# A two-layer decoder trunk: half of the low parts of the FFN output weights are subtracted on GpSimd instead of VectorE

## The chip, the cores and the metric

The kernel runs on one core of a Trainium2 chip. The metric is the device time of one execution in microseconds, as the median of several runs. One execution was also taken by the hardware profiler, and all rows below come from it. The engines are called as in the profile: PE is TensorE (PEld its weight loads), DVE is VectorE, ACT is ScalarE, POOL is GpSimd, SP is SyncE, whose queue (SPq) issues the loads of weights.

## The reference

256 tokens of 1024 fp32 values pass through two layers. Each layer is half an FFN, a token mixer, and half an FFN again, each with a norm before and a norm after it and added to the residual. The mixer of the first layer is stick-breaking attention, that of the second latent attention. The FFN is the part that the change touches:

```python
def swiglu(x, w_in, w_out):
    gate, up = jnp.split(x @ w_in, 2, axis=-1)
    return (jax.nn.silu(gate) * up) @ w_out
...
    for i in range(DEPTH):
        g = norm_g[i]
        f = swiglu(rms_norm(x, g[0]), ffn_w_in[i, 0], ffn_w_out[i, 0])
        x = x + FFN_RESIDUAL_WEIGHT * rms_norm(f, g[1])
        ...
        f = swiglu(rms_norm(x, g[4]), ffn_w_in[i, 1], ffn_w_out[i, 1])
        x = x + FFN_RESIDUAL_WEIGHT * rms_norm(f, g[5])
```

`w_in` is 1024 by 5632, `w_out` 2816 by 1024, all in fp32. There are four FFNs.

## The kernel before

**Pieces.** Every weight is read once from HBM, in the order in which it is used, into one of four raw tiles of 128 by 1024 fp32 (`RAWS`; `load`, line 329; the queue is SyncE's, its loads are line 334). A raw tile holds two pieces, 128 rows of a weight by 512 columns. ACT rounds a piece to fp32r, its high part (`nc.scalar.copy`, line 345); DVE subtracts that from the raw values, which gives the low part (`low`, line 351). A raw tile is free for the next load when both subtractions are done. High and low parts lie in `r` tiles, of which there are 76.

**Products.** For each piece PE does three products of 512 columns: high by high, high by low and low by high (`mm3`, line 476; the product itself is line 474). The tokens are two blocks of 128, and each uses every piece, so a piece is used by two times three products. Block 0 goes ahead of block 1 by at most `LEADS` pieces (14 in the first FFN), and at most `CAPS` pieces are held split (28 there).

**The FFN** (`ffn`, line 617). The inner dimension goes in 11 steps j of 256. For a step PE sums 8 pieces of gate and up columns into one bank. ACT does the silu (line 634), DVE multiplies it by the up half (line 636, the tile is `w`, called `hid` in the source), PE transposes that (line 482), ACT and DVE split it (lines 492 and 512), and the output rows of step j - 1 are added to two accumulator banks. The output rows of a step are 256 rows of `w_out`: two raw tiles of 128 rows by 1024 columns, and so four pieces, with key `("out", l, f, j, k, n)`, where k is the half of the rows and n the half of the columns. `add_rows` makes them in the order (k, n) = (0, 0), (0, 1), (1, 0), (1, 1); only the last group of all goes by n first.

**Norms.** POOL does little: constants at the start, four memsets, some copies in the latent attention, and the power -1/2 of each norm on one column (line 544; `rpre` for the norm ahead of a sub-layer, `rpost` for that behind it). Behind `rpost` DVE adds to the residual (line 581) and PE transposes the result for the next sub-layer (line 482).

**The order.** Nothing is ordered at run time. `Plan` records operations with their engine, a duration that the author gave, a class, and what they read and write. `run` then does a list schedule: an engine takes the operation that can start first, class 0 ahead of class 1 (the splits and the piece products are of class 1). The order that comes out is the program; each engine works through its own queue in that order, and waits at an instruction until what it reads is there and what it writes is free. A changed duration or engine can thus move instructions anywhere behind it.

Of the kernel before, what the change touches and what calls it, by code (L numbers as in the profile page):

```python
# [41 lines left out]
# For each sub-layer: how many pieces the first block of tokens may lead by, how many may be held.  # L42
# [14 lines left out]
# Durations, in microseconds, by which the order of the instructions is chosen.  # L57
# [23 lines left out]
class Buf:  # L81
    """A tile of a pool; it takes a slot with its first operation and gives it back after its last."""
# [17 lines left out]
class Plan:  # L100
    """Operations with what they read and write; run() emits them in the order of a list schedule."""
# [39 lines left out]
    def alt(self, o, eng, us, fn):  # L141
        """Another engine that may take the operation."""
        o.alt[eng] = (us, fn)
# [13 lines left out]
    def bank_ready(self, o, eng):  # L157
        """Two engines never access one bank at the same time."""
        w = 0.0
        for b in o.bufs:  # L160
            if b.tag == "bank":
                for e, end in b.touch.items():
                    if e != eng:
                        w = max(w, end + CROSS)
        return w
# [90 lines left out]
class Piece:  # L256
    """128 rows of a weight by up to 512 of its columns: the moving operand of three matrix products."""
# [7 lines left out]
def trunk(ctx: ExitStack, tc: tile.TileContext, x, positions, norm_g, ffn_w_in, ffn_w_out,  # L265
# [19 lines left out]
    # ---------------------------------------------------------------- constants  # L285
# [23 lines left out]
    # The tensor engine's clock rises with use: it is kept busy until the first operands are there.  # L309
# [14 lines left out]
    # ---------------------------------------------------------------- stream of weights  # L324
# [4 lines left out]
    def load(loads):  # L329
        """loads: (view of the raw tile, source, bytes)."""  # L330
# [8 lines left out]
    def split(raw, key, off, n, ks):  # L339
# [13 lines left out]
        op("dve", dve_us(n), low, r=rr + [(pc.hi, 0)], w=[(pc.lo, 0)], cls=1)  # L353

    def add(loads, parts):
        """parts: (key, offset, columns, loads it reads)."""
# [15 lines left out]
    def add_in2(kind, w, c0, c1, n):  # L372
        """[1024, n] at c0 beside [1024, n] at c1."""
# [50 lines left out]
    # ---------------------------------------------------------------- the tokens, and the gains of the norms  # L424
# [47 lines left out]
    # ---------------------------------------------------------------- helpers  # L472
# [11 lines left out]
    def act_hi(dst, src, n, r, w, scale=None, fast=False):  # L484
        """A copy, rounded, by ACT, or from SBUF (fast) by whichever engine is free first; dst, src: functions
        that give the access patterns once the buffers are placed."""
# [31 lines left out]
    def split_halves(dst, n, src, r):  # L518
        """src to both halves of a 512-column buffer: high part, low part."""
# [17 lines left out]
    def rstd(srcs, ss, ms, r, scale, eps, cls=0):  # L537
        """srcs: two functions giving halves of 512 columns, with what they read."""
# [8 lines left out]
    def pre_norm(b, l, i):  # L547
        """Gives x * gain, transposed, in two parts; the norm's factor, one per token, goes to rpre."""
# [36 lines left out]
    def use(b, key, fn, o, r, n):  # L585
        """The products of one piece of a weight."""
# [8 lines left out]
    def project(b, key, width):  # L595
        """[tokens, width] of x @ w, without the norm's factor."""
# [10 lines left out]
    def out_rows(b, key, t, acc, first, last, by_half=False):  # L607
        """acc += t^T @ w for 256 rows of w; t: a buffer of high and low parts."""
# [7 lines left out]
    # ---------------------------------------------------------------- FFN  # L616
# [35 lines left out]
    # ---------------------------------------------------------------- stick-breaking attention  # L652
# [3 lines left out]
    def tiles(b):  # L656
        """A bank of scores for four heads, or for two: (pair of heads, block of keys)."""
# [140 lines left out]
    # ---------------------------------------------------------------- rotary tables  # L798
# [8 lines left out]
    def rope_tables():  # L807
        """cos and sin of position * frequency: the angle in turns, taken apart so that every product
        whose whole turns are dropped is exact."""
# [327 lines left out]
```

## Time and profile before

| | |
|---|---|
| median of 2 runs | 970.34 us (970.26 to 970.42) |
| span of the profiled execution | 968.2 us; what lies around the span is not in the profile (the runs are 2.1 us longer) |
| granted TensorE clock, mean | 0.999 of full speed |
| HBM read | 168.15 MB, 175 GB/s over the span |

The span goes from the first to the last instruction. An idle time is put down to the engine that ended it, by the semaphores. Starts of instructions are good to the hundredth of a microsecond or so; the ends of products are modelled, since PE works on several at a time, so a product seems longer (some 390 ns) than the distance to the next one.

### The profile page before, as it was taken

How to read it: one execution, taken by the hardware profiler on the slowest of the kernel's cores; microseconds unless marked ns; L12 is line 12 of the kernel's file. 1: busy time of each engine (PE TensorE's matmuls, PEld its weight loads, DVE VectorE, ACT ScalarE, POOL GpSimd, SP SyncE). 2: the span in 40 equal slices, each digit the busy share in tenths (PEclk: the TensorE clock that was granted, in tenths of full speed). 3: DMA queues.
4: the chain of work that ended last, by engine and by line, in shares of the span. 5: the costliest groups of instructions: out<-in, count | busy, mean ns of one | idle time of the engine just before them, and what ended most of it. 6: DMA issues, size and time to landing. Idle time of an engine off the chain costs nothing.

```text
span 968.2 us, 13457 instructions
## 1 busy us (share of the span) xinstructions
PE 956.9 (99%) x4575; PEld 797.1 (82%) x4575; DVE 643.3 (66%) x1214; ACT 562.7 (58%) x1202; POOL 26.2 (3%) x75
## 2 busy tenths in 40 slices
PE   8999999999999999999999999999999999999997
PEld 6778888888888888888888888888899988888885
DVE  7884646678777875645477564556899997555533
ACT  7754535568878764545364453545798776444421
POOL 2000000000000000000000000000200000000000
PEclk9999999999999999999999999999999999999999
DMA  8885665634434385656745656575614178666511
GB/s 276 280 249 184 193 199 184 207 131 153 131 109 153 112 276 176 193 180 188 225 131 174 190 184 192 179 232 168 192 41 131 32 236 278 196 194 188 186 62 44
DMA packets 127974, 170.10 MB, mean 176 GB/s; under 512 B 8768, under 2 KB 109472, under 8 KB 127904
## 3 DMA queue, kind: packets, MB, share of 16 engines
q1 hardware_dynamic: 127792, 169.18, 55.2%
q8 instruction: 36, 0.59, 0.3%
q14 instruction: 34, 0.28, 0.1%
q10 hardware_dynamic: 112, 0.05, 0.0%
HBM read 168.15 MB, written 1.05 MB: 175 GB/s over the span
## 4 chain that ended last, share of the span: by engine, by line
PE 92%; DMA 3%; DVE 2%; ACT 1%; issue 1%; POOL 0%; SPq 0%; DVEq 0%; POOLq 0%; ACTq 0%
PE bank L474 88%; PE bank L482 5%; DMA raw<-in_ffn_w_in_dram 3%; DVE r L351 2%; ACT r L345 1%; SPq L334 0%; DVE w L636 0%; DVE w L559 0%; ACT r L492 0%; DVE x L581 0%; DVEq L1133 0%; ACT junk L540 0%; POOLq L1133 0%; POOL cbuild L299 0%; POOL invf L818 0%
## 5 line engine op out<-in xcount | busy, mean ns | idle before, releaser
L474 PE MATMUL bank<-r,r 128*128 128x512 f32 (+3 forms) x4080 | 926.2, 384 | 0.3 <-ACT r L345 0.2
L474 PEld LDWEIGHTS bank<-r,r 128*128 128x128 f32 (+1 forms) x4080 | 736.7, 188 | 139.5 <-ACT r L345 1.2
L351 DVE TENSOR_TENSOR r<-raw,r 128x512 fp32r<-128x512 f32 (+1 forms) x628 | 400.1, 683 | 42.4 <-ACT r L345 33.1
L345 ACT CAST r<-raw 128x512 fp32r<-128x512 f32 (+1 forms) x628 | 353.9, 616 | 56.8 <-DMA raw<-in_ffn_w_in_dram 26.7
L634 ACT ACTIVATE w<-bank,rpre 128x256 f32<-128x256 f32 x88 | 41.7, 474 | 215.5 <-PE bank L474 215.4
L636 DVE SCALAR_TENSOR_TENSOR w<-bank,rpre,w 128x256 f32<-128x256 f32 x88 | 42.5, 483 | 185.9 <-ACT w L634 185.9
L492 ACT CAST r<-bank 128x256 fp32r<-128x256 f32 (+5 forms) x166 | 64.2, 399 | 75.6 <-PE bank L482 65.7
L512 DVE TENSOR_TENSOR r<-bank,r 128x256 fp32r<-128x256 f32 (+5 forms) x166 | 74.3, 454 | 45.8 <-ACT r L492 44.7
L482 PE MATMUL bank<-ident,w 128*128 128x128 f32 (+1 forms) x326 | 55.0, 272 | 2.1 <-DVE w L636 2.0
L482 PEld LDWEIGHTS bank<-ident,w 128*128 128x128 f32 (+1 forms) x326 | 41.3, 137 | 16.6 <-DVE w L636 4.0
L512 DVE TENSOR_TENSOR r<-w,r 128x512 fp32r<-128x512 f32 x48 | 32.5, 687 | 4.9 <-ACT r L507 2.0
L540 ACT ACTIVATE junk<-bank 128x512 bf16<-128x512 f32 x24 | 14.3, 597 | 22.6 <-PE bank L474 22.5
L578 DVE TENSOR_TENSOR w<-bank,w 128x512 f32<-128x512 f32 x24 | 16.4, 684 | 15.9 <-ACT junk L540 15.7
L544 POOL TENSOR_TENSOR rpost<-ms,half_neg 128x1 f32<-128x1 f32 x12 | 6.6, 548 | 700.0 <-DVE ms L542 700.0
L559 DVE TENSOR_TENSOR w<-bank,gT 128x512 f32<-128x512 f32 x24 | 16.3, 686 | 2.2 <-PE bank L482 2.0
L540 ACT ACTIVATE junk<-x 128x512 bf16<-128x512 f32 x24 | 15.1, 631 | 4.3 <-DVE x L581 2.3
L581 DVE SCALAR_TENSOR_TENSOR x<-w,rpost,x 128x512 f32<-128x512 f32 x24 | 17.1, 745 | 0.4
L482 PE MATMUL bank<-ident,x 128*128 128x128 f32 x96 | 15.0, 297 | 0.0
L482 PEld LDWEIGHTS bank<-ident,x 128*128 128x128 f32 x96 | 12.9, 155 | 1.9 <-issue 0.2
L492 ACT CAST r<-w 128x512 fp32r<-128x512 f32 x20 | 12.2, 619 | 3.6 <-DVE w L559 3.5
L1035 ACT ACTIVATE w<-bank,mx 128x128 f32<-128x128 f32 (+1 forms) x32 | 13.1, 425 | 0.4 <-DVE mx L1031 0.3
L736 DVE SCALAR_TENSOR_TENSOR w<-bank,w 128x512 f32<-128x512 f32 x12 | 8.2, 689 | 4.3 <-ACT w L734 4.1
(85 smaller groups left out, 211.5 us busy)
## 6 DMA issues: line engine op xcount, KB each, us to landing
raw<-in_ffn_w_in_dram SPq DMA_DIRECT2D x352, 256.0 KB, 3.9
raw<-in_ffn_w_out_dram SPq DMA_DIRECT2D x88, 512.0 KB, 4.3
raw<-in_sb_w_in_dram SPq DMA_DIRECT2D x32, 256.0 KB, 3.6
raw<-in_sb_w_in_dram SPq DMA_DIRECT2D x8, 512.0 KB, 4.7
raw<-in_sb_w_out_dram SPq DMA_DIRECT2D x8, 512.0 KB, 3.3
raw<-in_mla_w_out_dram SPq DMA_DIRECT2D x8, 512.0 KB, 3.9
w<-in_norm_g_dram SPq DMA_DIRECT2D x12, 256.0 KB, 4.8
raw<-in_mla_w_in_dram SPq DMA_DIRECT2D x4, 416.0 KB, 3.6
```

Of the source, the lines that this page charges most:

```text
L345: h = op("act", act_us(n), lambda: nc.scalar.copy(pc.hi[:, :n], raw[:, off:off + n]), r=rr, w=[(pc.hi, 0)], cls=1, after=splits[-1:], piece=i)
L351: nc.vector.tensor_tensor(out=pc.lo[:, :n], in0=raw[:, off:off + n], in1=pc.hi[:, :n].bitcast(F32), op=ALU.subtract)
L474: nc.tensor.matmul(o, a, b, start=start, stop=stop, skip_group_check=True)
L482: nc.tensor.transpose(o, i, ident[:])
L492: nc.scalar.copy(dst(), src())
L512: nc.vector.tensor_tensor(out=dst(), in0=src(), in1=hi().bitcast(F32), op=ALU.subtract)
L540: op("act", act_us(512, 1), lambda src=src, h=h: nc.scalar.activation(junk[:], src(), AF.Square, scale=scale, accum_out=ss[:, h:h + 1]), r ...
L559: op("dve", dve_us(512), lambda h=h, y=y, tr=tr: nc.vector.tensor_tensor(out=y[:].rearrange("p (k t) -> p k t", t=P), in0=tr[:].rearrange( ...
L578: op("dve", dve_us(512), lambda h=h, t=t: nc.vector.tensor_mul(out=t[:], in0=acc[h][:], in1=g[h][:]), r=[(acc[h], 0), (g[h], 0)], w=[(t, 0 ...
L581: op("dve", dve_us(512) + 0.06, lambda h=h, t=t: nc.vector.scalar_tensor_tensor(xt[b][h][:], t[:], k.rpost[:], xt[b][h][:], op0=ALU.mult, ...
L634: op("act", act_us(FT, 1), lambda o=o, hid=hid: nc.scalar.activation(hid[:, 0:FT], o[:, 0:FT], AF.Silu, scale=k.rpre[:]), r=[(o, 0), (k.rp ...
L636: op("dve", dve_us(FT) + 0.06, lambda o=o, hid=hid: nc.vector.scalar_tensor_tensor(hid[:, FT:], o[:, FT:], k.rpre[:], hid[:, 0:FT], op0=AL ...
```

## The change

In `split`, a piece whose key begins with `out` and ends with 1, that is the second half of the columns of the FFN output rows, gets its low part from POOL: the same subtraction on the same tiles, given to the planner with 1.4 us instead of `dve_us(512)`, which is 0.60 us, in the same class. Output rows of the two attentions have other keys and stay as they were. Comments and docstrings go too, so lines behind line 351 move by six; nothing else changes.

```diff
         def low():
             nc.vector.tensor_tensor(out=pc.lo[:, :n], in0=raw[:, off:off + n], in1=pc.hi[:, :n].bitcast(F32),
                                     op=ALU.subtract)
-        op("dve", dve_us(n), low, r=rr + [(pc.hi, 0)], w=[(pc.lo, 0)], cls=1)
+        def low_pool():
+            nc.gpsimd.tensor_tensor(out=pc.lo[:, :n], in0=raw[:, off:off + n], in1=pc.hi[:, :n].bitcast(F32),
+                                    op=ALU.subtract)
+        if key[0] == "out" and key[-1] == 1:
+            op("pool", 1.4, low_pool, r=rr + [(pc.hi, 0)], w=[(pc.lo, 0)], cls=1)
+        else:
+            op("dve", dve_us(n), low, r=rr + [(pc.hi, 0)], w=[(pc.lo, 0)], cls=1)
```

On DVE, the first group of output rows stood like this before (lines 351 are the subtractions, `r43` to `r48` the low parts of the group from `raw0` and `raw1`, line 512 the split of `hid`, line 636 the next `hid`):

```order
L512 TENSOR_TENSOR r37_98<-bank2_152,r37_98 128x256
L351 TENSOR_TENSOR r39_100<-raw3_149,r36_97 128x512
L351 TENSOR_TENSOR r41_102<-raw3_149,r38_99 128x512
L351 TENSOR_TENSOR r43_104<-raw0_146,r40_101 128x512
L351 TENSOR_TENSOR r45_106<-raw0_146,r42_103 128x512
L351 TENSOR_TENSOR r47_108<-raw1_147,r44_105 128x512
L351 TENSOR_TENSOR r48_109<-raw1_147,r46_107 128x512
L636 SCALAR_TENSOR_TENSOR w7_144<-bank1_151,rpre0_198,w7_144 128x256
```

Now DVE has this there (`rt` are small steps of the rotary tables; lines are six higher behind line 351):

```order
L518 TENSOR_TENSOR r37_98<-bank2_152,r37_98 128x256
L351 TENSOR_TENSOR r39_100<-raw3_149,r36_97 128x512
L351 TENSOR_TENSOR r41_102<-raw3_149,r38_99 128x512
L351 TENSOR_TENSOR r43_104<-raw0_146,r40_101 128x512
L836 TENSOR_SCALAR rt9_232<-rt8_231 128x32
L837 TENSOR_SCALAR rt4_227<-rt4_227 128x32
L837 TENSOR_SCALAR rt9_232<-rt9_232 128x32
L847 SCALAR_TENSOR_TENSOR rt5_228<-rt4_227,rt3_226 128x32
L351 TENSOR_TENSOR r47_108<-raw1_147,r45_106 128x512
L842 TENSOR_SCALAR rt11_234<-rt4_227 128x32
L847 SCALAR_TENSOR_TENSOR rt22_245<-rt4_227,rt21_244 128x32
L642 SCALAR_TENSOR_TENSOR w7_144<-bank1_151,rpre0_198,w7_144 128x256
```

The second subtraction of each of the two raw tiles is gone from DVE, and steps of the rotary tables that stood further back have taken their room.

On POOL, at the change from the second FFN to the third (501 to 513 us in the trace of before), the powers of the two norms of both blocks stood one behind the other before. Now subtractions stand between them (lines 550 are the powers, line 354 the subtractions):

```order
L354 TENSOR_TENSOR r71_132<-raw2_148,r10_71 128x512
L354 TENSOR_TENSOR r31_92<-raw3_149,r15_76 128x512
L550 TENSOR_TENSOR rpost0_195<-ms0_194,half_neg_161 128x1
L354 TENSOR_TENSOR r0_61<-raw0_146,r48_109 128x512
L550 TENSOR_TENSOR rpre0_198<-msx0_197,half_neg_161 128x1
L354 TENSOR_TENSOR r39_100<-raw1_147,r46_107 128x512
L550 TENSOR_TENSOR rpost1_201<-ms1_200,half_neg_161 128x1
L550 TENSOR_TENSOR rpre1_204<-msx1_203,half_neg_161 128x1
```

A power thus waits for the subtraction ahead of it, and `rpost1`, behind which the residual of block 1 stands, has one directly before it.

On PE the order of the products and transposes is the same up to the end of the third FFN but for one place at the start, where the transposes of a `hid` stand three products later. From the end of the third FFN through the latent attention it differs. There, before (lines 482 are the transposes of the residual of block 0):

```order
L474 MATMUL bank6_156<-r44_105,r3_64 128x512
L482 MATMUL bank5_155<-ident_158,x0_188 128x128 x4
L482 MATMUL bank0_150<-ident_158,x0_188 128x128 x4
L474 MATMUL bank6_156<-r37_98,r73_134 128x512
L474 MATMUL bank6_156<-r69_130,r73_134 128x512
L474 MATMUL bank6_156<-r37_98,r3_64 128x512
```

and now:

```order
L480 MATMUL bank6_156<-r44_105,r6_67 128x512
L488 MATMUL bank5_155<-ident_158,x0_188 128x128 x4
L480 MATMUL bank6_156<-r37_98,r68_129 128x512
L480 MATMUL bank6_156<-r70_131,r68_129 128x512
L480 MATMUL bank6_156<-r37_98,r6_67 128x512
L488 MATMUL bank0_150<-ident_158,x0_188 128x128 x4
```

The second half of the transposes has gone behind the three products of a piece; behind this place the orders part further.

## Rows read from the trace of the kernel before

**Rows 1.** The page: busy us, share of the span, instructions of each engine

```profile
PE 956.9 (99%) x4575; PEld 797.1 (82%) x4575; DVE 643.3 (66%) x1214; ACT 562.7 (58%) x1202; POOL 26.2 (3%) x75
```

**Rows 2.** The chain that ended last, in order of time: start, us, what

```profile
373.18 11.59 PE bank L474 x51
...
390.00 11.59 PE bank L474 x51
```

**Rows 3.** Waits of PE: who for whom, us in total, times, longest

```profile
PE bank L482 <- DVE w L636: 2.0, 3, 1.2
```

**Rows 4.** Stretches: length; busy us (x) of PE, PEld, DVE, ACT, POOL; clock, DMA share, GB/s

```profile
20.00:62.00 42.00, 40.50 (x182) 32.57 (x180) 35.04 (x96) 27.33 (x55) 0.00 (x0) 1.00 0.86 280
...
680.00:790.00 110.00, 110.00 (x667) 98.95 (x666) 102.89 (x238) 90.79 (x250) 10.43 (x20) 1.00 0.35 110
```

**Rows 5.** Groups of instructions: busy us, mean ns, idle before it and its releasers

```profile
L351 DVE TENSOR_TENSOR r<-raw,r 128x512 fp32r<-128x512 f32 x612 | 391.9, 686 | 41.8 <-ACT r L345 32.4 <-ACT w L731 0.6 <-PE bank L474 0.6
```

**Rows 6.** Groups of instructions of POOL

```profile
L544 POOL TENSOR_TENSOR rpost<-ms,half_neg 128x1 f32<-128x1 f32 x12 | 6.6, 548 | 700.0 <-DVE ms L542 700.0
...
L628 POOL MEMSET r<- 128x512 f32 x4 | 2.0, 527 | 155.5 <-PE bank L474 155.5
...
L297 POOL MEMSET cbuild<- 128x128 f32 x4 | 0.8, 204 | 0.1
```

**Rows 7.** Stretches of line 474 (all products) alone: PE, PEld

```profile
0.00:46.00 46.00, 38.09 (x146) 27.43 (x147) 1.00 0.86 280
...
0.00:150.00 150.00, 141.42 (x587) 109.28 (x588) 1.00 0.71 227
```

**Rows 8.** Stretches of line 351 (low parts of pieces) alone: DVE

```profile
0.00:46.00 46.00, 25.00 (x40) 1.00 0.86 280
...
0.00:150.00 150.00, 75.07 (x118) 1.00 0.71 227
```

**Rows 9.** Waits in 0 to 64 us, of ACT and of the load queue

```profile
ACT r L345 <- DMA raw<-in_ffn_w_in_dram: 11.2, 9, 1.9
...
SPq L334 <- DVE r L351: 11.7, 13, 2.2
```

**Rows 10.** Timeline of the start: start us, us, engine, what, idle before it

```profile
23.08 2.87 ACT L345 CAST r<-raw 128x512 fp32r<-128x512 f32 x5
...
23.55 3.69 DVE L351 TENSOR_TENSOR r<-raw,r 128x512 fp32r<-128x512 f32 x6
...
35.33 0.44 PE L482 MATMUL bank<-ident,w 128*128 128x128 f32 x2 [0.34 <-DVE w L636]
...
42.72 1.15 ACT L345 CAST r<-raw 128x512 fp32r<-128x512 f32 x2 [1.00 <-DMA raw<-in_ffn_w_in_dram]
...
45.11 0.44 PE L482 MATMUL bank<-ident,w 128*128 128x128 f32 x2 [1.16 <-DVE w L636]
```

**Rows 11.** Timeline: two powers on POOL and what DVE did beside each

```profile
687.21 1.30 DVE L512 TENSOR_TENSOR r<-w,r 128x512 fp32r<-128x512 f32 x2
687.39 0.93 POOL L544 TENSOR_TENSOR rpre<-msx,half_neg 128x1 f32<-128x1 f32 x1 [3.71 <-DVE msx L542]
...
512.38 0.68 DVE L559 TENSOR_TENSOR w<-bank,gT 128x512 f32<-128x512 f32 x1
...
512.61 0.55 POOL L544 TENSOR_TENSOR rpre<-msx,half_neg 128x1 f32<-128x1 f32 x1 [3.49 <-DVE msx L542]
```

**Rows 12.** Timeline of the change from the second FFN to the third

```profile
500.92 2.17 ACT L345 CAST r<-raw 128x512 fp32r<-128x512 f32 x4
...
505.57 0.55 POOL L544 TENSOR_TENSOR rpre<-msx,half_neg 128x1 f32<-128x1 f32 x1 [4.02 <-DVE msx L542]
...
506.20 0.62 ACT L345 CAST r<-raw 128x512 fp32r<-128x512 f32 x1
...
508.57 0.55 POOL L544 TENSOR_TENSOR rpost<-ms,half_neg 128x1 f32<-128x1 f32 x1 [2.44 <-DVE ms L542]
...
511.01 1.03 PE L482 MATMUL bank<-ident,x 128*128 128x128 f32 x8
```

## Prediction

> **What bounds the kernel now.** I read the busy shares first, then TensorE's own waits, then the chain of waits, and only then the engine that the change touches. TensorE (PE) is busy 99% of the span of 968.2 us and VectorE (DVE) 66% [rows 1]. A busy share alone can hide a queue that crawls, so the chain matters more: within an FFN the same pattern returns from 373.18 to 390.00 us [rows 2], that is every 16.82 us. In that time the code issues 48 products for the gate and up columns of both blocks, 24 for the output rows and 4 transposes, 76 in all, with hardly a gap. TensorE waits for DVE's product `hid` 2.0 us in three waits, the longest 1.2 us [rows 3]. Those three waits lie in the first 63 us. In the stretch 20 to 62 us, 182 products started [rows 4]; at 76 per 16.82 us there would be 190, so 8 are missing, at 0.22 us each some 1.7 us. Everywhere else TensorE sets the time. So the change, which takes work from DVE, can give back about 2 us at the start and nothing more; what it can cost is a new wait of TensorE.
>
> **The subtractions that move.** There are 44 groups of output rows (4 FFNs of 11), four pieces each, two of them with the second half of the columns: 88 subtractions. DVE's take 686 ns each [rows 5], so DVE loses 60 us of its 643. By the chain none of it lay on the path outside the start, so this alone is worth nothing there.
>
> The trace shows no two-input POOL (GpSimd) instruction on 512 columns. Bounds from the nearest rows [rows 6]: a memset of 512 columns took 527 ns, and it reads nothing, so the subtraction is not shorter. From 128 to 512 columns the memset grew by 323 ns, 0.84 ns a column, or 0.43 us for one pass of 512. Two reads and a write passed one after the other are 1.29 us, and on top of the 548 ns of a one-column two-input POOL instruction that makes 1.84 us. I take the middle, 1.2 us. In the Trainium skill, the GPSIMD Engine Reference (3.1, elementwise cycle accounting) gives 4497 ns for a two-input add of 2048 fp32 columns; a quarter is an estimate of 1.12 us, which no run here shows, and with it the sum below would fall by about 0.1 us.
>
> **What hides it in the steady part.** Count how far the split parts are ahead. By 150 us TensorE had started 587 products of the product line [rows 7]; less the 8 that warm it up, and by three, that is 193 uses of pieces by both blocks. Block 0 may lead by 14 at most in this FFN, so it had used at most (193 + 14) / 2 = 103. DVE had made 118 low parts [rows 8], 14 pieces ahead. Twelve pieces take 16.82 us, so a low part lies ready some 20 us before it is read. Half a microsecond more on POOL, or even 3 us, vanishes in that. By 46 us, with 146 products, the count is (46 + 14) / 2 = 30 used at most against 40 made: already 10 ahead. POOL's load is 2 x 1.2 us in 16.82 us. If the cover were gone each moved piece would cost its extra 0.5 us, 88 x 0.5 = 44 us; the count says that it isn't.
>
> **The start.** Here the stream of weights is the limit: casts wait 11.2 us for the loads, and the queue of loads waits 11.7 us for DVE's subtractions to give back one of the four raw tiles [rows 9]. So what counts is when the low parts of a raw tile are finished. Take the first output group. Five casts run from 23.08 for 2.87 us [rows 10], 0.57 us each; the third is the moved piece of `raw0`, done at 24.8, the fifth that of `raw1`, done at 25.95. DVE's six subtractions from 23.55 take 0.615 us a step, so the two moved ones, fourth and sixth, end at 26.0 and 27.24. On POOL, if nothing holds it up, the first runs 24.8 to 26.0 and the second to 27.2: both raw tiles come back when they did. DVE's freed time goes to small rotary-table steps that the planner put there, as the order shows. So without contention the start changes by 0.
>
> But POOL and DVE don't seem independent. The one-column power took 930 ns at 687.39, while DVE ran subtractions with both inputs in SBUF from 687.21, and 0.55 us at 512.61, while DVE read one input from PSUM [rows 11]. The first DVE instruction there ends near 687.9; 687.39 + 0.93 is 0.4 us after that, as if POOL had to wait for it. If each then waits for the other, DVE's third subtraction ends at 25.4, POOL runs 25.4 to 26.6, DVE's next to 27.3, POOL's second to 28.5: `raw0` comes back 0.6 us late and `raw1` 1.26 us. The rule is stated in the Trainium skill, SBUF — State Buffer (Who interferes with whom): a DVE instruction with two SBUF inputs and a GpSimd instruction that reads SBUF share one read interface, and the second one blocks until the first is done. By that rule the start costs up to 1.26 us a group, without it nothing; the power's row agrees with the rule, and whether DVE also waits for POOL no run here shows yet.
>
> Ends for the start: -2.0 us (TensorE's three waits go) to +5.0 us (four groups before 62 us, each 1.26 us late, all of it passed on through the four tiles). I take +1.0, nearest to the first group's row: one such delay, since DVE and the casts sit idle for the loads between groups and take up the rest. The transposes of `hid` that TensorE waited for at 35.33 now stand three products later; that removes a wait of 0.34 us [rows 10], but the loads then decide the next one at 45.11, so I count it as nothing.
>
> **The norms on POOL.** POOL now holds subtractions between the powers of the norms at 501 to 513 us, and it runs in order: a power stands behind a subtraction, which waits for its cast and for a free tile. The casts were made early (four from 500.92), so the first subtraction runs at about 503 to 504.5 and the power at 505.57 is not late. The power at 508.57 stands behind a cast made at 506.2 to 506.8, so a subtraction from 506.8 to about 508.0: 0.5 us of room. Behind that power the residual of block 1 waits, and behind the residual its transposes at 511.01 [rows 12], without room of their own. Ends: 0 and +1.3 us (one whole subtraction in the way); I take +0.1. The other powers have no moved piece near them, or come where block 1 has plenty left.
>
> **The latent attention.** No piece of it moves, but the planner's times do, and from the end of the third FFN TensorE's order changes. DVE is busy 102.89 of 110 us there and TensorE 110.00 [rows 4]. An order can't win where TensorE has no gap, so the low end is 0; the longest wait of TensorE for another engine in the trace of before was 1.2 us [rows 3], and two or three of these are +3. I take +0.2, nearest to the row that shows none.
>
> **Sum.** Against the profiled execution: 968.2 + 1.0 + 0.1 + 0.2 = 969.5 us of span. The median of the runs is 970.34, 2.1 us over the span (start and end of the execution). So 970.34 + 1.3 = 971.6 us, +0.1%. A measurement of this kernel can tell about 2% from no change, 19 us: this is no change.
>
> **Rivals.** First, the raw tiles (slower): with POOL and DVE waiting for each other, every output group at the start returns its tiles 1.26 us late and nothing takes it up: 4 x 1.26 = 5.0, so 975.4 us. For it: the power's 930 ns and the queue's 11.7 us. Against it: the gaps in which DVE waits for casts. It decides if the subtraction takes over about 1.2 us and DVE's neighbours stretch. Chance 0.17.
>
> Second, relief: DVE's 8 fewer subtractions in the first 62 us let `hid` come sooner, and the three waits go: 970.34 - 2.0 = 968.3. For it: all three waits name DVE. Against it: at 45.11 the product came late because ScalarE's queue sat behind a cast at 42.72 that waited for a load. Chance 0.13.
>
> Third, the reordered attention leaves TensorE uncovered twice or thrice: +3 there and +1.0 at the start, 974.3. Chance 0.08.
>
> Fourth, POOL becomes the bound: two subtractions in 16.82 us do so from 8.4 us each; at 9 us, 44 x (18 - 16.82) = 52 us, so 1022. It would need seven times my figure. It is also what would be slower by over 2% (from 8.6 us). Chance 0.02.
>
> **How the numbers follow.** The forecast, 970 to 973.5, has 0.60. With the rivals at 968.3 and 975.4 inside, the range is 968.2 to 976.0. Faster by 2% is not to be had, since TensorE's own gaps sum to some 2 us: 0.01. Slower by 2%: the fourth rival and a little for what I don't see, 0.03. Within 2%: 0.96.
>
> **What would show it.** POOL: 88 subtractions near 1.2 us, longer beside DVE's two-input ones; DVE busy near 583 us; the pattern of 16.82 us unchanged; TensorE's waits for `hid` before 63 us between 0 and 5 us; none named POOL. The forecast is wrong if TensorE waits for POOL inside an FFN, if the pattern lengthens, or if 680 to 790 us shows gaps of over 3 us.

## The result, and the profile after

The changed kernel took 976.33 us, the median of 2 runs (975.16 to 977.49), against 970.34. The ratio to before is 1.0064, interval 1.0042 to 1.0085: 0.6% slower. That is within the 2% that were called no change, but it lies 0.33 us above the range of 968.2 to 976.0, and 4.7 us above the number. The profiled execution is the slower of the two, 977.49 us with a span of 975.8 us, 7.6 us more than the span before. Lines behind 351 are six higher than in the rows of before.

The page's busy line, which answers to [rows 1], already holds the first surprise:

```profile
PE 958.8 (98%) x4575; PEld 795.7 (82%) x4575; DVE 637.2 (65%) x1126; ACT 563.8 (58%) x1206; POOL 151.1 (15%) x163
```

DVE has 88 instructions fewer, 60 us by the mean of [rows 5], and yet its busy time fell by 6 us only, from 643.3 to 637.2. POOL's grew by 125 us. The groups of DVE and POOL show why (busy us, mean ns of one, idle time before it and what ended it):

```profile
L351 DVE TENSOR_TENSOR r<-raw,r 128x512 fp32r<-128x512 f32 x524 | 381.6, 768 | 58.0 <-ACT r L345 50.4 <-ACT w L737 0.6 <-PE bank L480 0.6
...
L642 DVE SCALAR_TENSOR_TENSOR w<-bank,rpre,w 128x256 f32<-128x256 f32 x88 | 42.4, 482 | 175.0 <-ACT w L640 175.0
...
L354 POOL TENSOR_TENSOR r<-raw,r 128x512 fp32r<-128x512 f32 x88 | 124.8, 1429 | 509.4 <-ACT r L345 406.3 <-DVE w L642 49.5 <-DMA raw<-in_ffn_w_out_dram 45.5
```

The 524 subtractions that stayed on DVE take 768 ns in the mean, where they took 686: 43 us more. The product `hid` of line 642, which reads one input from PSUM, still takes 482 ns. POOL's subtractions range from 1.275 us to 1.91, with a median of 1.296. The 524 fall into two kinds: the 82 that run while one of POOL's does take 1.21 us in the mean, the 442 others 0.69 us.

One place in the timeline shows what happens inside such a pair (start, us, what):

```profile
48.40 1.28 POOL L354 TENSOR_TENSOR r<-raw,r 128x512 fp32r<-128x512 f32 x1 [9.03 <-ACT r L345]
48.44 0.42 DVE L518 TENSOR_TENSOR r<-bank,r 128x256 fp32r<-128x256 f32 x1
...
48.78 1.46 DVE L351 TENSOR_TENSOR r<-raw,r 128x512 fp32r<-128x512 f32 x1
```

POOL's subtraction ends at 49.68. DVE's of line 518, one input from PSUM, runs beside it in its usual 0.42 us. DVE's of line 351, both inputs from SBUF, starts at 48.78 and ends at 50.24, that is 0.56 us after POOL's end. Where DVE's subtractions run one behind the other, one ends every 0.60 us (eight in 4.90 us from 786.98 in the trace of before). So it stood still until POOL was done and then did about one pass. No wait is shown for this: the time is booked as DVE being busy.

**Where it costs nothing.** The chain within an FFN, against [rows 2]:

```profile
375.88 11.58 PE bank L480 x51
...
392.69 11.60 PE bank L480 x51
```

The pattern returns after 16.81 us, as before. DVE is held up here as well, but the split parts lie ready.

**Where it costs.** I cut both executions at the same four events, powers `rpost` on POOL that stand at the end of the first FFN, of the second, of the latent attention and of the last FFN, each for one block. The columns are length, busy us and count of PE, PEld, DVE, ACT, POOL, then clock, DMA share and GB/s. Before:

```profile
0.00:191.09 191.09, 186.34 (x823) 150.53 (x824) 123.89 (x253) 106.35 (x211) 7.75 (x42) 1.00 0.69 222
191.09:501.01 309.92, 309.92 (x1497) 259.20 (x1496) 210.87 (x370) 195.94 (x395) 4.70 (x9) 1.00 0.54 168
501.01:780.73 279.72, 279.72 (x1438) 238.80 (x1437) 203.39 (x412) 174.01 (x423) 11.53 (x23) 1.00 0.50 156
780.73:957.99 177.26, 177.12 (x805) 145.74 (x804) 99.96 (x174) 84.99 (x173) 1.09 (x2) 1.00 0.54 174
```

After:

```profile
0.00:193.19 193.19, 186.23 (x823) 149.79 (x824) 117.17 (x231) 106.42 (x211) 36.96 (x64) 0.99 0.69 219
193.19:503.70 310.51, 310.19 (x1497) 259.17 (x1496) 206.07 (x348) 195.89 (x395) 34.30 (x30) 1.00 0.54 168
503.70:786.11 282.41, 281.41 (x1439) 238.52 (x1438) 206.94 (x391) 175.29 (x427) 44.70 (x44) 1.00 0.49 155
786.11:965.59 179.48, 177.18 (x804) 145.44 (x803) 101.90 (x151) 84.84 (x172) 34.08 (x24) 1.00 0.55 171
```

The idle time of PE is the length less PE's busy time:

| stage | longer | of it PE idle | of it PE busy |
|---|---|---|---|
| first FFN | +2.10 | +2.21 | -0.11 |
| first attention, second FFN | +0.59 | +0.32 | +0.27 |
| third FFN, latent attention | +2.69 | +1.00 | +1.69 |
| last FFN | +2.22 | +2.16 | +0.06 |
| sum | +7.60 | +5.69 | +1.91 |

So PE stands idle longer in the first and in the last FFN, by 2.2 us each, and by 1.0 us in the stretch with the third FFN and the latent attention. In that stretch PE is also shown busy for longer, with one product more. The waits of PE name the engine at fault, against [rows 3]:

```profile
PE bank L488 <- DVE w L642: 4.4, 4, 1.9
PE bank L480 <- DVE r L351: 2.2, 3, 1.0
```

It is DVE, not POOL. No wait of PE's products names POOL's subtraction; one weight load does, for 0.5 us at the start. Of the 2.2 us for low parts, 1.04 us are the wait at 28.75, shown below; the other two waits, at 9.1 and 24.4 us, end before POOL's first subtraction at 24.93. The row of the load queue that [rows 9] has with 11.7 us now has 15.6, and one of POOL's stands beside it (stretch 0 to 64 us):

```profile
SPq L334 <- DVE r L351: 15.6, 16, 3.0
...
SPq L334 <- POOL r L354: 1.9, 2, 1.1
```

That is no longer wait for the raw tiles as a whole: the profile puts other waits of this queue down to rotary steps and to `hid`, and all its rows that name DVE or POOL come to 33.9 us before and to 31.0 us now.

The first output group, whose times the prediction worked out from [rows 10], went like this:

```profile
24.93 3.04 POOL L354 TENSOR_TENSOR r<-raw,r 128x512 fp32r<-128x512 f32 x2 [12.72 <-DMA raw<-in_ffn_w_out_dram]
...
25.47 1.27 DVE L836 TENSOR_SCALAR rt<-rt 128x32 f32<-128x32 f32 x1
...
26.66 1.35 DVE L837 TENSOR_SCALAR rt<-rt 128x32 f32<-128x32 f32 x2
...
28.02 0.68 DVE L351 TENSOR_TENSOR r<-raw,r 128x512 fp32r<-128x512 f32 x1
...
28.75 0.73 PE L480 MATMUL bank<-r,r 128*128 128x512 f32 x2 [1.04 <-DVE r L351]
```

The rotary steps that moved into DVE's freed place are 32 columns long and take 0.17 us elsewhere. Beside POOL one took 1.27 us. Two such stops put the remaining subtraction behind them to 28.02, and PE waits for it. POOL's first subtraction ended at 26.70, after 1.78 us: it had begun beside one of DVE's, which ended at 25.55.

The stretch 790 to 820 us, which the prediction did not look at, is the last FFN, where `hid` is late in the same way:

```profile
792.06 2.40 DVE L518 TENSOR_TENSOR r<-w,r 128x512 fp32r<-128x512 f32 x2
...
792.47 3.12 POOL L354 TENSOR_TENSOR r<-raw,r 128x512 fp32r<-128x512 f32 x2 [0.96 <-ACT r L345]
...
793.86 0.47 ACT L640 ACTIVATE w<-bank,rpre 128x256 f32<-128x256 f32 x1
...
794.38 1.75 DVE L351 TENSOR_TENSOR r<-raw,r 128x512 fp32r<-128x512 f32 x1
796.05 0.47 DVE L642 SCALAR_TENSOR_TENSOR w<-bank,rpre,w 128x256 f32<-128x256 f32 x1
...
796.58 0.44 PE L488 MATMUL bank<-ident,w 128*128 128x128 f32 x2 [1.88 <-DVE w L642]
```

The silu is done at 794.33, but `hid` stands behind a subtraction that takes 1.75 us, some 1.07 us too long, and PE waits 1.88 us for the transposes' input. Before, in the stretch 790 to 820 us PE was busy 29.86 of 30 and the loads ran at 298 GB/s; now it is 27.70 and 232 GB/s (the stretch lies 5.4 us earlier in the work).

### The profile page after: what moved, and what is told of

Same layout as the page of the kernel before. It is cut to its first block, busy times and chain, and to the rows that moved or that the text cites. A ratio compares the mean times of both kernels' runs of the same rounds, so it can differ in the third digit from the quotient of the medians.

```text
span 975.8 us, 13671 instructions
## 1 busy us (share of the span) xinstructions
PE 958.8 (98%) x4575; PEld 795.7 (82%) x4575; DVE 637.2 (65%) x1126; ACT 563.8 (58%) x1206; POOL 151.1 (15%) x163
## 4 chain that ended last, share of the span: by engine, by line
PE 87%; DVE 5%; DMA 4%; ACT 2%; issue 1%; POOL 0%; SPq 0%; DVEq 0%; POOLq 0%; ACTq 0%
PE bank L480 83%; PE bank L488 4%; DMA raw<-in_ffn_w_in_dram 3%; DVE r L351 2%; ACT r L345 1%; DVE r L518 1%; ACT junk L546 1%; DVE w L565 1%; DMA w<-in_norm_g_dram 0%; DMA raw<-in_ffn_w_out_dram 0%; POOL r L354 0%; DVE rt L847 0%; DVE rt L836 0%; ACT r L498 0%; SPq L334 0%
## 5 line engine op out<-in xcount | busy, mean ns | idle before, releaser
L480 PE MATMUL bank<-r,r 128*128 128x512 f32 (+2 forms) x4080 | 927.7, 384 | 3.0 <-DVE r L351 2.2
L351 DVE TENSOR_TENSOR r<-raw,r 128x512 fp32r<-128x512 f32 (+2 forms) x540 | 390.6, 764 | 58.9 <-ACT r L345 51.3
L354 POOL TENSOR_TENSOR r<-raw,r 128x512 fp32r<-128x512 f32 x88 | 124.8, 1429 | 509.4 <-ACT r L345 406.3
L550 POOL TENSOR_TENSOR rpre<-msx,half_neg 128x1 f32<-128x1 f32 x12 | 8.0, 665 | 71.3 <-DVE msx L548 71.3
```

Of the source, the lines that this page charges most:

```text
L351: nc.vector.tensor_tensor(out=pc.lo[:, :n], in0=raw[:, off:off + n], in1=pc.hi[:, :n].bitcast(F32), op=ALU.subtract)
L354: nc.gpsimd.tensor_tensor(out=pc.lo[:, :n], in0=raw[:, off:off + n], in1=pc.hi[:, :n].bitcast(F32), op=ALU.subtract)
L480: nc.tensor.matmul(o, a, b, start=start, stop=stop, skip_group_check=True)
```

## The experiments

The theory after the result: POOL's subtraction and a DVE instruction with both inputs in SBUF exclude each other (theory A), and the time that DVE loses reaches PE where no split parts lie in stock. Against it stood three rivals. The order: the planner's new order alone costs the time (theory B). The late tile: a raw tile simply comes back later because POOL needs 1.3 us where DVE needed 0.69 (theory D in what follows). The rotary steps: DVE's queue is held only because the planner put those short steps beside POOL.

**Order alone.** The planner still thinks that POOL does it, so every engine has the changed kernel's order, but DVE does the subtraction.

```diff
-            op("pool", 1.4, low_pool, r=rr + [(pc.hi, 0)], w=[(pc.lo, 0)], cls=1)
+            op("pool", 1.4, low, r=rr + [(pc.hi, 0)], w=[(pc.lo, 0)], cls=1)
```

> The order of the changed kernel on every engine, but DVE does the 88 subtractions at the places where POOL's stood in the program. Theory A (POOL and DVE exclude each other while both read SBUF, and what stands behind the blocked DVE instruction is late): the waits of PE near 28, 45 and 794 us shrink to at most those of before; what the new order of the attention costs stays (about 2 us), so 970.5 to 972.5 us. Theory B (the new order of the instructions costs the time): the time stays at 975 to 977.5 us. Theory D (POOL's subtraction is only longer, so raw tiles come back late): as A.

972.21 us against 970.56, ratio 1.0020 (1.0006 to 1.0033). So the order costs 1.65 us of the 6, with 0.6 to 3.2 us by the interval. The stretches cut at the same powers:

```profile
0.00:189.49 189.49, 185.00 (x823) 148.75 (x824) 123.58 (x253) 106.40 (x211) 7.75 (x42) 1.00 0.70 224
189.49:781.04 591.55, 591.29 (x2935) 497.70 (x2934) 414.49 (x782) 371.62 (x821) 16.89 (x31) 1.00 0.52 162
781.04:958.74 177.70, 177.16 (x804) 145.50 (x804) 99.27 (x173) 84.67 (x172) 1.09 (x3) 1.00 0.55 172
```

The middle stretch was 309.92 + 279.72 = 589.64 us before: 1.91 us more, of which only 0.26 is idle time of PE. The rest is PE shown busy for longer, as in the changed kernel. One product more falls into the stretch (it has 2934 before, taken as one), which is 0.2 us. The ends of products are modelled, so what the other 1.4 us are is not to be read from these rows. The first FFN is 1.60 us shorter here than before, and this execution was the shortest of its ten, so the rows don't hold the whole 1.65 us and don't show where it lies.

**Engine alone.** The opposite: the order of before on every engine, but the instruction goes to POOL.

```diff
-            op("pool", 1.4, low_pool, r=rr + [(pc.hi, 0)], w=[(pc.lo, 0)], cls=1)
+            op("dve", dve_us(n), low_pool, r=rr + [(pc.hi, 0)], w=[(pc.lo, 0)], cls=1)
```

> The order of the kernel before on every engine, but POOL does the 88 subtractions. Theory A: DVE instructions beside POOL's take up to 1.3 us longer, PE waits at the start and near 790 us as in the changed kernel, the attention (680 to 785 us) has no new gaps: 972.5 to 975 us. Theory B: 970.3 us, within 1 us.

976.35 us, 1.0066 (1.0044 to 1.0087): the whole loss, without the new order, and above the 972.5 to 975 us that theory A had expected. By the medians the two parts do not add: 1.65 and 5.8 us are more than the 6.0 of the changed kernel; the intervals (4.3 to 8.4 us here) leave that open. The rotary steps stand where they stood before, so they are not needed for the loss. PE's wait for `hid`, and the two stretches behind the first FFN:

```profile
PE bank L488 <- DVE w L642: 7.8, 7, 1.8
...
191.44:783.80 592.36, 590.90 (x2934) 497.59 (x2933) 413.67 (x737) 369.85 (x816) 78.53 (x74) 1.00 0.52 162
783.80:964.41 180.61, 177.39 (x805) 145.61 (x804) 102.54 (x152) 85.11 (x173) 33.67 (x24) 1.00 0.55 171
```

The first FFN is 0.35 us longer than before, the middle 2.72 and the last FFN 3.35. Of the middle 1.46 us are idle time of PE, and 1.4 of it three waits at 352, 513 and 518 us, at the starts of the second and third FFN. The other 1.26 us are PE shown busy for longer, with the same products in the same order. The changed kernel's middle is 3.28 us longer, so its loss there need not be the new order's alone.

**POOL that only writes.** POOL does three memsets (512, 512 and 256 columns) in the place of the subtraction, about as long as it.

```diff
-            nc.gpsimd.tensor_tensor(out=pc.lo[:, :n], in0=raw[:, off:off + n], in1=pc.hi[:, :n].bitcast(F32),
-                                    op=ALU.subtract)
+            for c in (n, n, n // 2):
+                nc.gpsimd.memset(pc.lo[:, :c].bitcast(F32), 0.0)
```

> The changed kernel in its own order, but POOL fills the low part with zeros in three memsets (512, 512 and 256 columns, by the rows of before 0.53 + 0.53 + 0.3 = 1.35 us, as long as the subtraction): POOL is as busy and reads nothing. The low parts of these pieces are left out. Theory A (reads exclude each other): DVE's subtractions go back to 0.686 us, 970.5 to 973 us. If any access of POOL blocks DVE, or if POOL's duration alone is what costs (theory D), or the order (theory B): 975 to 977.5 us.

971.25 us, 1.0011 (1.0000 to 1.0022). In the page's busy line and in the groups DVE's subtractions are back at their old duration, with POOL busy at the same time:

```profile
PE 957.8 (99%) x4575; PEld 797.2 (82%) x4575; DVE 591.9 (61%) x1126; ACT 563.2 (58%) x1206; POOL 146.1 (15%) x339
...
L351 DVE TENSOR_TENSOR r<-raw,r 128x512 fp32r<-128x512 f32 x524 | 341.0, 689 | 70.8 <-ACT r L345 63.3 <-ACT w L737 0.6 <-PE bank L480 0.6
...
L355 POOL MEMSET r<- 128x512 f32 x176 | 93.0, 528 | 447.2 <-PE bank L480 437.2 <-ACT r L345 4.9
```

129 of DVE's subtractions run beside a memset, at 0.69 us in the mean. The memsets need not wait for the raw tile and do not hold it, so this run leaves theory D alive.

**Not at the starts, planned so.** The first four steps of the first and of the last FFN go back to DVE, in the planner too; 72 of 88 stay on POOL.

```diff
-        if key[0] == "out" and key[-1] == 1:
+        if key[0] == "out" and key[-1] == 1 and not (key[1] == key[2] and key[3] < 4):
```

> POOL subtracts as in the changed kernel, but not in the first four groups of output rows of the first and of the last FFN, where loads are late; 72 subtractions stay on POOL. Theory A: the waits near 28, 45 and 794 us go, those of the attention (about 2 us) and single ones near 353 and 513 us (1.2 us together) stay: 971.5 to 973.5 us. Theory B: the order of PE is that of the changed kernel but for one place, so 975 to 977.5 us.

973.15 us against 970.56, 1.0030 (1.0019 to 1.0040): 2.6 us of loss are left. PE's order is the changed kernel's but for one place, so the order's own cost is in these 2.6 us beside that of the 72; the runs in the order of before, below, separate them.

**Rotary steps out of the way.** The positions are loaded later, so the rotary steps do not stand at the start. In the changed kernel, and the same edit in the kernel before:

```diff
-           w=[(pi, 0)], cls=2, after=stream[3:4])
+           w=[(pi, 0)], cls=2, after=stream[45:46])
```

> The changed kernel, with the rotary tables' first load put behind the 46th load of weights instead of the fourth, so their small DVE steps and two ScalarE sines run after 100 us. Theory A in the form that the blocked DVE queue is the path (a rotary step of 0.17 us took 1.27 us beside POOL and hid stood behind it): the start gains 1.5 to 3 us, 973 to 975 us. If late raw tiles are the path (theory D), the start stays: 975.5 to 977 us.

> The kernel before with the same move of the rotary tables. It takes some 10 us of small DVE steps out of the start, where loads are the limit: 969 to 970.6 us by either theory; at 968.5 or below it would beat both kernels.

The changed kernel: 977.64 us, 1.0073 (1.0054 to 1.0091), no better. The kernel before: 968.98 us, 0.9994 (0.9978 to 1.0010), the same. So the rotary steps as the cause fall: DVE's subtractions take 776 ns in the mean without them. Theory A in the form written down here, with the held rotary steps as the path, had expected 973 to 975 us and missed. Theory D's 975.5 to 977 us lies nearest, so by these expectations the run points to the late tiles, whatever makes them late.

**POOL that reads one column.** As the run that only writes, but behind two memsets POOL subtracts one column, so it does read the raw tile and holds it. The planner's duration is the same.

```diff
-            nc.gpsimd.tensor_tensor(out=pc.lo[:, :n], in0=raw[:, off:off + n], in1=pc.hi[:, :n].bitcast(F32),
+            for c in (n, n):
+                nc.gpsimd.memset(pc.lo[:, :c].bitcast(F32), 0.0)
+            nc.gpsimd.tensor_tensor(out=pc.lo[:, :1], in0=raw[:, off:off + 1], in1=pc.hi[:, :1].bitcast(F32),
```

> The changed kernel in its own order; POOL writes the low part by two memsets of 512 columns (1.05 us) and then subtracts one column alone, so it holds the raw tile until some 1.3 us after the cast as before, but reads one column. The other low columns of these pieces are left out. Theory A (the read of POOL blocks DVE): 970.5 to 972.5 us, as without any read. Theory D (the raw tile comes back late): 975 to 977 us, as the changed kernel.

970.81 us, 1.0009 (0.9997 to 1.0021): the loss is gone, with 2 x 528 + 239 ns = 1.30 us of POOL for each piece. That was meant to bring theory D down, and doesn't do it alone: the memsets wait for no cast, so they mostly ran ahead of it, and the tile was held for the 239 ns of the one column only. What the run does show is DVE beside a busy POOL, its subtractions at 688 ns in the mean. The timeline at the first group:

```profile
25.48 0.63 DVE L838 TENSOR_SCALAR rt<-rt 128x32 f32<-128x32 f32 x1
25.55 1.11 POOL L355 MEMSET r<- 128x512 f32 x2
...
26.34 0.69 DVE L351 TENSOR_TENSOR r<-raw,r 128x512 fp32r<-128x512 f32 x1
```

A subtraction of DVE runs in 0.69 us beside POOL's memset, but a rotary step of 32 columns, one input and both sides in SBUF, took 0.63 us instead of 0.17. So the two kinds of DVE work are held by different things: the two-input one not by a POOL that only writes, the short one by that too, though not each time (others beside a memset took 0.17 us).

**Late steps only, in the order of before.** POOL does the subtraction only from step 4 of each FFN on: 56 of 88.

```diff
-        if key[0] == "out" and key[-1] == 1:
-            op("pool", 1.4, low_pool, r=rr + [(pc.hi, 0)], w=[(pc.lo, 0)], cls=1)
+        if key[0] == "out" and key[-1] == 1 and key[3] >= 4:
+            op("dve", dve_us(n), low_pool, r=rr + [(pc.hi, 0)], w=[(pc.lo, 0)], cls=1)
```

> The order of the kernel before; POOL subtracts only in steps j of 4 and more of each FFN (56 of the 88), where split parts lie 8 to 20 us ahead. Theory A: the block of DVE is still there (subtractions up to 1.4 us) but hidden: 970.0 to 971.3 us. If the block costs time in the steady part too, 64% of the 5.8 us: 974 us.

969.97 us, 1.0006 (0.9992 to 1.0019): nothing. And DVE is held there as elsewhere:

```profile
385.00 1.29 POOL L354 TENSOR_TENSOR r<-raw,r 128x512 fp32r<-128x512 f32 x1 [50.61 <-ACT r L345]
385.47 1.37 DVE L351 TENSOR_TENSOR r<-raw,r 128x512 fp32r<-128x512 f32 x1 [0.62 <-ACT r L345]
```

DVE ends at 386.84, 0.55 us after POOL. With stock ahead that reaches nobody.

**Starts only, in the order of before.** POOL does only the first four steps of the first and last FFN: 16 of 88.

```diff
-        if key[0] == "out" and key[-1] == 1:
-            op("pool", 1.4, low_pool, r=rr + [(pc.hi, 0)], w=[(pc.lo, 0)], cls=1)
+        if key[0] == "out" and key[-1] == 1 and key[1] == key[2] and key[3] < 4:
+            op("dve", dve_us(n), low_pool, r=rr + [(pc.hi, 0)], w=[(pc.lo, 0)], cls=1)
```

> The order of the kernel before; POOL subtracts only in the first four groups of output rows of the first and of the last FFN: 16 of the 88. Theory A (the block costs time only where TensorE has no stock): most of the 5.8 us that the engine alone cost, 974 to 976 us. If every blocked DVE instruction costs alike: 16/88 of it, 971.6 us.

973.98 us against 969.39, 1.0044 (1.0030 to 1.0057): 4.6 of the 5.8 us come from 16 of the 88. By difference 1.2 us are left for the 16 at the starts of the second and third FFN, less than the noise of the two runs, but near the 1.4 us that PE waited there with the engine alone. The timeline at the last FFN:

```profile
788.81 2.99 POOL L354 TENSOR_TENSOR r<-raw,r 128x512 fp32r<-128x512 f32 x2 [1.48 <-ACT r L345]
788.85 5.90 DVE L351 TENSOR_TENSOR r<-raw,r 128x512 fp32r<-128x512 f32 x6
792.41 2.93 SPq L334 DMA_DIRECT2D raw<-in_ffn_w_in_dram  x6
...
796.30 1.14 ACT L345 CAST r<-raw 128x512 fp32r<-128x512 f32 x2 [2.29 <-DMA raw<-in_ffn_w_in_dram]
...
797.35 0.47 ACT L640 ACTIVATE w<-bank,rpre 128x256 f32<-128x256 f32 x1
...
798.70 0.44 PE L488 MATMUL bank<-ident,w 128*128 128x128 f32 x2 [1.61 <-DVE w L642]
```

Six subtractions of DVE take 5.90 us where 0.615 us a step, as the prediction read at the start, would give 3.7. This place tells the block from theory D: POOL's two end at 791.80 and DVE's last at 794.75, so the last tile comes back with DVE's. By theory D, without a block, POOL would end at about 788.81 + 2 x 1.29 = 791.4, DVE at 788.85 + 3.7 = 792.55, and POOL's length would delay nothing. The first tile of the six comes back with DVE's second subtraction, which ends at 792.35 after 1.78 us, and its load starts at 792.41, 2.2 us later in the work than before. ACT waits 2.29 us for it, and the silu stands behind those casts in ACT's queue. PE then waits for `hid`, and the profile names DVE, although DVE had only passed the delay on. This is a second way from the same cause to PE, beside DVE's own queue at 794.38 us above. A share of theory D is not excluded: at the start of the engine-alone run the load queue waits 7.0 us in all for POOL's subtractions.

**A fifth raw tile.** If late tiles were the main way, one tile more should take up most of it. `WSLOTS` goes down to make room. Once with DVE doing all the subtractions, once with POOL in the same order:

```diff
-WSLOTS = 9
-RAWS = 4
+WSLOTS = 7
+RAWS = 5
...
-            op("pool", 1.4, low_pool, r=rr + [(pc.hi, 0)], w=[(pc.lo, 0)], cls=1)
+            op("dve", dve_us(n), low, r=rr + [(pc.hi, 0)], w=[(pc.lo, 0)], cls=1)
```

> Five raw tiles instead of four and seven w tiles instead of nine, all subtractions on DVE; the planner orders some of the attention anew. The loads run further ahead: 968 to 971 us by either theory. It is the base for the next.

The second has `low_pool` in the last line instead of `low`.

> The order of the kernel with five raw tiles, but POOL does the 88 subtractions. If the block reaches TensorE by way of the loads (a blocked subtraction gives its raw tile back late), a fifth tile takes most of it up: less than 3 us over the kernel with five tiles on DVE. If it reaches TensorE by way of DVE's queue (hid stands behind the blocked instruction): 4 to 6 us over it, as with four.

968.89 us, 0.9989 (0.9980 to 0.9999) with DVE, and 973.81 us, 1.0042 (1.0029 to 1.0056) with POOL. The difference is 4.9 us, where it was 5.8 with four tiles. So the fifth tile takes up about a sixth at most; the 0.9 us are within the noise. As late tiles by POOL's own length should have gone with it, this too speaks against theory D as the main cause. By the expectation the 4.9 us speak for DVE's own queue as the way to PE, while the run with late rotary steps spoke for the late loads; how the loss divides between the two, these runs do not settle.

The first of the two is a little faster than both kernels. Its stretch of 20 to 62 us, against that of [rows 4]:

```profile
20.00:62.00 42.00, 41.95 (x191) 33.88 (x190) 38.51 (x107) 29.46 (x61) 0.00 (x0) 1.00 0.91 305
```

PE is busy 41.95 of 42 us there, with 305 GB/s of loads. That is the gain at the start which the prediction's second rival hoped to get from POOL. The fifth tile is the likely reason, but the `w` tiles and the order changed with it. The first FFN ends at 187.24 instead of 191.09 us in this profile, and most of that is given back behind it.

**Fifth tile and late rotary steps in the kernel before.** Both small gains together:

```diff
-WSLOTS = 9
-RAWS = 4
+WSLOTS = 7
+RAWS = 5
...
-           w=[(pi, 0)], cls=2, after=stream[3:4])
+           w=[(pi, 0)], cls=2, after=stream[45:46])
```

> The version that the runs point to: no subtraction on POOL, five raw tiles, seven w tiles, and the rotary tables after 100 us. If their two gains (about 0.5 us for five tiles, about 0.6 us for the tables) add up, 968.0 to 969.2 us, 0.1 to 0.2% under the kernel before; if both only fill the same gaps of the start, no more than the five tiles alone, 968.9 us.

970.36 us against 970.07, 1.0002 (0.9993 to 1.0011). They do not add. PE's order is that of the run with five tiles, so a new order of PE is not the reason; the reason stays open.

## Why the prediction was wrong

**The step that failed.** The prediction had the mutual waiting of POOL and DVE in view and priced it as one delayed tile at the first group, +1.0 us. It let idle time between groups take up the rest of the start, and put the starts of the other FFNs at nothing. The engine alone, in the order of before, costs 5.8 us, and 4.6 us come from the 16 subtractions at the starts of the first and last FFN.

**The steady part: right.** The pattern of 16.82 us stayed (16.81), and PE's products wait for POOL nowhere in an FFN. The run of the late steps alone shows it directly: 56 of 88 on POOL, no loss. Counting how many split parts lie ready was a sound way to cost an edit at nothing.

**DVE's busy time: wrong.** I took 60 us from DVE's 643 and named 583 as what would show it. It is 637.2. Two errors are in that. One is in the sum: subtractions that run one behind the other overlap a little, so 88 fewer give back 51 us and not 60; where POOL only writes, DVE is busy 591.9 us. The other is the 45 us above that, 41 of them in the group of line 351 (381.6 against 341.0). This is where the error came from: I asked whether DVE and POOL hold each other only for the first group of output rows, as a delay of one tile, and not as a price on all DVE work near a POOL subtraction. The power's 0.93 us in [rows 11] had shown POOL waiting for DVE; the runs show DVE waiting for POOL in the same way. Both lose by it, POOL 12 us (88 at 1.429 us instead of 1.296) and DVE more. The Trainium skill's rule in SBUF — State Buffer (Who interferes with whom), that a DVE instruction with two SBUF inputs contends with a GpSimd instruction that reads SBUF and not with one that only writes, agrees with the groups of the runs: 768 and 775 ns in the mean where POOL subtracts, 689 and 688 ns where it writes, or writes and reads one column.

**POOL's duration: a little off.** Taken as 1.2 us, measured as 1.296 in the median, 1.43 in the mean with the waits for DVE in it. It lies within the bounds of 0.53 to 1.84. The estimate of 1.12 us from the Trainium skill, GPSIMD Engine Reference (3.1, elementwise cycle accounting), is below the shortest of the 88, 1.275 us.

**The start: sign right, size off.** I took +1.0 with ends of -2.0 and +5.0, and the profiled execution lost 2.1 us in the first FFN. In the first group the mutual waiting went as it had been worked out: `raw0` came back with POOL's first subtraction at 26.70 and `raw1` with DVE's last at 28.70, 0.66 and 1.46 us later than before, where 0.6 and 1.26 were forecast. What failed is that idle time takes up the rest: PE waited 1.04 us for that low part itself, and 1.78 us for a `hid` at 46.84 (1.16 before). The prediction had counted ten split parts ahead there; that stock covers the products, and not `hid`, which stands in DVE's queue. Some 1.3 us of the 2.1, by the estimate at the end, are the lower clock of this one execution; it fits that PE is busy 186.23 us here and 185.00 in the run with the order alone, which has the same order. Two kernels with the same instructions in the first four steps, before and the one with POOL in the late steps only, end the first FFN at 191.09 and 190.09 us, so a single profile is good to about 1 us in this term; three with POOL there end it at 193.19, 191.44 and 192.58.

**The last FFN: missing.** No term of the sum stood for it, since the rows of [rows 3] put all waits for `hid` in the first 63 us. But a place with no wait is not a place with stock. In the changed kernel it cost 2.2 us, with the engine alone 3.35, and with the start it makes most of the loss: 4.6 of 5.8 us in the run of the starts alone. The starts of the second and third FFN were put at nothing in the same way, and cost PE 1.4 us of waits with the engine alone.

**The attention's order: mis-sized.** I took +0.2, with 0 as the low end and +3 as the high one, nearest to the row without gaps. Order alone costs 1.65 us in the runs (0.6 to 3.2), with hardly a gap to be seen: the 110 us from 680 on still show PE busy 109.28 in the changed kernel. Looking for gaps of over 3 us there, as the prediction asked, would have missed it. That the attention is the place is likely, since PE's order hardly differs elsewhere, but no row shows it.

**The norms' powers: +0.1, and no wait by the way that was named.** What answers to [rows 12] on POOL:

```profile
505.93 1.70 POOL L354 TENSOR_TENSOR r<-raw,r 128x512 fp32r<-128x512 f32 x1 [1.68 <-ACT r L345]
508.20 0.56 POOL L550 TENSOR_TENSOR rpre<-msx,half_neg 128x1 f32<-128x1 f32 x1 [0.57 <-DVE msx L548]
509.59 1.34 POOL L354 TENSOR_TENSOR r<-raw,r 128x512 fp32r<-128x512 f32 x1 [0.84 <-ACT r L345]
512.29 0.55 POOL L550 TENSOR_TENSOR rpost<-ms,half_neg 128x1 f32<-128x1 f32 x1 [1.35 <-DVE ms L548]
```

POOL stands idle 0.57 and 1.35 us before the two powers, so neither waited for the subtraction ahead of it. PE waits 0.3 us for the residual of block 1 there, where it waited for nothing before; DVE ends that wait, not POOL.

**The rivals.** The first, tiles and mutual waiting, 975.4 us, came nearest in number and in mechanism, and its own condition was met: POOL took over 1.2 us and its neighbours stretched. It had the place half right. It counted four groups at the start and none at the last FFN, and it let the delay pass through the tiles alone, while a fifth tile takes up only 0.9 of 5.8 us. The engine alone, at 976.35 us, already lies past the upper end of the range, so the new order is not needed to explain that. The second, relief, did not come: DVE's freed time was gone before it could be used, and where DVE did get its time back, with POOL that only writes, the kernel took 971.25 us. The third was right that the new order costs, without the two or three long waits that it named. The fourth was far off, as its chance of 0.02 said.

## What to carry to other kernels

Before moving an elementwise operation from DVE to POOL, ask what DVE runs beside it. Here DVE's two-input work in SBUF stood still while POOL read there, and 45 of the 51 us that the move would have freed came back, booked as busy. Ask of an edit not what share of the time its engine is busy, but at which places the engine behind it has no stock: 16 of 88 instructions at two starts cost 4.6 us, and 56 in the middle nothing. To tell a new order from a new engine, let the planner keep the old entry and emit the instruction on the other engine, and the reverse.

## What the runs showed that was not expected

A rotary step of 32 columns took 1.27 us beside POOL's subtraction and 0.63 us beside POOL's memset, against 0.17 us alone. Beside the same memset a two-input subtraction of 512 columns kept its 0.69 us.

The profiled execution of the changed kernel lost clock once, behind a wait of PE of 1.78 us for `hid` that ended at 46.84 us (stretch, as above):

```profile
48.00:52.00 4.00, 4.00 (x12) 3.24 (x13) 4.00 (x8) 2.51 (x6) 2.56 (x2) 0.57 0.76 242
```

The granted clock of 0.57 means that for most of these 4 us it was at 1.2 and not 2.4 GHz. Twelve products and transposes ran there, where the steady pattern, 76 in 16.82 us, has 18; at 0.22 us each the six are 1.3 us. The other execution had a mean clock of 0.999 instead of 0.997 and was 2.3 us shorter. A longer wait in the run of the starts alone, 2.3 us, was not followed by a lower clock, so what decides it stays open here.
